# Order of the first loads and of a's first transposes in a two-matmul kernel with GELU between

## The chip, the cores and the metric

The kernel runs on one core of a Trainium2 chip. The metric is the device time of one execution in microseconds, as the median of several executions; smaller is better. A core has a matrix engine (TensorE, PE in the profile, with its weight loads as PEld), three engines for elementwise work (VectorE or DVE, ScalarE or ACT, GpSimd or POOL), and SyncE (SP), which here only issues transfers. Each engine runs its own instructions in order and waits for others at semaphores. Sixteen transfer (DMA) engines move data between the chip's main memory and the on-chip memory SBUF. TensorE writes its results to PSUM, of which there are eight banks of 128 partitions by 512 float32.

## The reference

```python
m, k, n, p = 1024, 1024, 2048, 1024        # a: m x k, b: k x n, c: n x p, float32
h = np.matmul(a, b)
h = 0.5 * h * (1 + np.tanh(np.sqrt(2 / np.pi) * (h + 0.044715 * h ** 3)))
return np.matmul(h, c).astype(np.float32)
```

## The kernel before

The order of all instructions is written out by hand; no scheduler moves them. `a` and `b` are turned into bfloat16. The first product is made transposed, as `hT = gelu(b^T a^T)`, so that TensorE needs `b` as it lies (its weights, 128 by 128) and `a` transposed (`aT`, streamed in 512 columns). `a`'s 1024 rows are two halves of 512 (index h), the contraction of 1024 is eight slices of 128 (index k), and the columns of `b` are tiles of 128 (index t): the first 1024 in `b1`, the others in `b2`. Much later parts, the function `seven` that is used for the rest of the first product and for the second one, multiply blocks of matrices with seven block products in place of eight. They are not touched by the change.

The change is in the start of the kernel, here called phase one: tiles t = 0 to 6 of `b1` against the first half of `a`, over the first half of the contraction, k = 0 to 3. It holds seven PSUM banks open, one for each t, and goes through k from outside, so 7 matmuls of 512 columns follow each slice of `b`, 28 in all (line 128). The eighth bank (7) is for transposes.

Phase one gets its data in float32 over SP's queue. `load_a(k, n)` (L71) brings n slices of 128 columns of `a` for its first 512 rows: 256 KB for one slice in rows of 512 bytes, 512 KB for two in rows of 1024 bytes. `load_b(k, c0, w)` (L74) brings slice k of `b`, `w` of its first 1024 columns: 512 KB, or 256 KB for a half. Eight transfers of 3 MB in all go out without any wait, in the order of lines 76 to 83: a0, the two halves of b0, a1, b1, a2 with a3, b2, b3.

What becomes of them:

- `turn0(k, n)` (L116): DVE casts n slices of `a` to bfloat16 (L118), TensorE transposes them in blocks of 128 by 128 into bank 7 (L122, four for each slice), and DVE copies the bank to `aT` (L124).
- ACT casts the first 512 columns of a slice of `b` (L135; for k = 0 in two pieces of 256), DVE the other 512 (L136).
- TensorE runs seven matmuls (L128) for each k. `turn0(0, 1)` stands ahead of k = 0, `turn0(1, 1)` after the seven of k = 0, `turn0(2, 2)` after the seven of k = 1.

All other loads are issued by POOL and cast to bfloat16 on the way. Ahead of them POOL runs one copy of one element, `gate` (L85), that reads `b`'s slice 1; so POOL's transfers begin when `load_b(1)` has landed. They are, in this order: `a10` and `a11`, the second 512 rows of `a` (L98, two transfers of 256 KB for each half of the contraction), the lower half of `b1` (L105, k = 4 to 7), `a01`, the first 512 rows of `a` for k = 4 to 7 (L98), the other half of `b` (`b2`, L109), and `c` (L112).

After phase one TensorE transposes `a10` (`turn`, L158, copied by DVE at L160), makes tile t = 7 of phase one, and goes on with the second half of `a` (L128 again). ACT and DVE move phase one's seven results to SBUF (`leave`, L147 and L149).

At the very start, ahead of everything, TensorE runs eight matmuls on zeros (L89).

Of the kernel before, what the change touches and what calls it, by code (L numbers as in the profile page):

```python
# [19 lines left out]
def kernel(ctx, tc, a, b, c, out):  # L20
# [22 lines left out]
    def bank(i, shape=(128, H), dt=F32, name="ps"):  # L43
        return pp.tile(list(shape), dt, name=name, tag=f"bank{i}", padded_shape=None)

    def pieces(tag, bufs, shape, dt, name):
        return small.tile(shape, dt, name=name, tag=tag, bufs=bufs)
# [19 lines left out]
    def slice_a(k, n):  # L67
        return sta[:, ds(k * H, n * H)].rearrange("p (mt c) -> p mt c", mt=4)

    def load_a(k, n):  # L70
        nc.sync.dma_start(out=slice_a(k, n), in_=av[:, 0:4, ds(k * 128, n * 128)])  # L71

    def load_b(k, c0=0, w=1024):
        nc.sync.dma_start(out=stb[:, k, ds(c0, w)], in_=bv[:, k, ds(c0, w)])  # L74

    load_a(0, 1)
    load_b(0, 0, H)
    load_b(0, H, H)
    load_a(1, 1)
    load_b(1)  # L80
    load_a(2, 2)
    load_b(2)
    load_b(3)

# [31 lines left out]
    def turn0(k, n):  # L116
        ab = pieces("ab", 2, [128, 4, n * 128], BF16, "ab")
        nc.vector.tensor_copy(ab, slice_a(k, n))  # L118
        pt = bank(7, (128, n, H), BF16, "pt")
        for i in range(n):  # L120
            for j in range(4):
                nc.tensor.transpose(pt[:, i, ts(j, 128)], ab[:, j, ts(i, 128)], ident)  # L122
        for i in range(n):
            nc.vector.tensor_copy(aT[:, 0, k + i], pt[:, i])  # L124

    def mm1(p, t, h, ks, k0=0, k1=KT):
        for k in ks:
            nc.tensor.matmul(p, b1[:, k, ts(t, 128)], aT[:, h, k],  # L128
                             start=(k == k0), stop=(k == k1 - 1))

    turn0(0, 1)
    for k in range(KH):
        for c0 in (0, 256) if k == 0 else (0,):
            w = 256 if k == 0 else H
            nc.scalar.activation(b1[:, k, ds(c0, w)], stb[:, k, ds(c0, w)], AF.Copy)  # L135
        nc.vector.tensor_copy(b1[:, k, H:], stb[:, k, H:])  # L136
        for t in range(N0):
            mm1(ps[t], t, 0, (k,), 0, KH)
        if k < 2:
            turn0(k + 1, k + 1)  # L140


    half = slot("x3", [128, 8, H], F32, "half")
# [268 lines left out]
```

## Time and profile before

| | |
|---|---|
| median of 11 runs | 122.7 us (121.83 to 125.36) |
| the profiled execution, whole | 122.23 us |
| its span in the profile | 120.5 us |
| TensorE matmuls busy | 112.7 us (94%) |
| TensorE weight loads busy | 71.7 us (60%) |
| DVE busy | 88.8 us (74%) |
| ACT busy | 50.8 us (42%) |
| POOL busy | 16.1 us (13%) |
| read from and written to main memory | 20.97 MB, 4.19 MB |

The first table line is the metric; the profile shows one execution, of 122.23 us, of which 120.5 us are the span between its first and its last instruction. Times in the profile are counted from the start of that span. Engines overlap, so busy times don't add up to the span. The profile's lines used below give, for a group of instructions on one engine, the start, the time from the first start to the last end, engine, line of the kernel, operation, what is written from what, the shape, the count, and in brackets how long the engine was idle before and which event ended that.

TensorE's waits before 30 us, as the profile sums them: 1.2 us for the zeros, 1.0 us in two waits for DVE's copies to `aT` (L124), 0.7 us for ACT's cast of `b` (L135), 0.4 us for DVE's cast of `b` (L136), and 0.5 us for the transfer of `a10`. POOL waits 8.7 us at the gate.

### The profile page before, as it was taken

What the parts mean: (1) busy time and instruction counts of PE and PEld (TensorE: products, weight loads), DVE (VectorE), ACT (ScalarE), POOL (GpSimd) and SP (SyncE); (2) the same over time, 40 slices, a digit from 0 to 9 for tenths busy, and PEclk for the clock granted to TensorE, in tenths of its full rate; (3) what the DMA queues carried; (4) which work ended last, traced back from release to release, by engine and by line L of the source; (5) the groups of instructions that cost most, each with busy time, mean ns of one, the idle gap of its engine ahead of it and who ended that gap; (6) DMA issues with size and microseconds to landing.
All of it is one profiled execution on the core that took longest, in us unless ns stands there. A gap on an engine that the chain in (4) does not pass through costs nothing.

```text
span 120.5 us, 1435 instructions
## 1 busy us (share of the span) xinstructions
PE 112.7 (94%) x536; PEld 71.7 (60%) x536; DVE 88.8 (74%) x97; ACT 50.8 (42%) x82; POOL 16.1 (13%) x29
## 2 busy tenths in 40 slices
PE   6787889999999999999999999999999999999970
PEld 2223445644644444888888444468888888888850
DVE  0224577498237899977779999969999996892490
ACT  4102461005537779946669536900012595100000
POOL 2006906853233000000000000000000000000000
PEclk9999999999999999999999999999999999999997
DMA  2899999999999999998000000062000002004695
GB/s 89 187 327 391 185 172 209 206 197 206 207 206 212 212 211 212 210 211 163 5 3 0 0 5 0 0 261 88 0 0 0 0 5 87 0 0 174 237 354 193
DMA packets 11110, 16.34 MB, mean 136 GB/s; under 512 B 736, under 2 KB 5856, under 8 KB 11104
## 3 DMA queue, kind: packets, MB, share of 16 engines
q0 software_dynamic: 6496, 8.91, 42.4%
q1 hardware_dynamic: 4608, 7.34, 17.6%
q8 instruction: 4, 0.07, 0.2%
q14 instruction: 2, 0.02, 0.0%
HBM read 20.97 MB, written 4.19 MB: 209 GB/s over the span
## 4 chain that ended last, share of the span: by engine, by line
PE 71%; DMA 16%; DVE 6%; SPq 1%; issue 1%; POOL 1%; ACT 1%; DVEq 0%; ACTq 0%
PE ps L229 50%; PE ps L128 18%; DMA stb<-in_b_dram 6%; DMA out_dram<-ot 5%; DMA a<-in_a_dram 5%; DVE x L187 4%; PE pt L158 2%; DVE ot L273 2%; SPq L74 1%; SPq L71 1%; POOL a L98 1%; DVE ot L358 1%; ACT u L268 1%; POOL gate L85 0%; DVEq L273 0%
## 5 line engine op out<-in xcount | busy, mean ns | idle before, releaser
L128 PE MATMUL ps<-aT,b 128*128 128x512 bf16 x128 | 30.6, 392 | 2.1 <-DVE aT L124 1.0
L229 PE MATMUL ps<-x,s 128*128 128x512 f32 x128 | 29.6, 391 | 0.0
L229 PEld LDWEIGHTS ps<-x,s 128*128 128x128 f32 x128 | 24.0, 188 | 5.1
L128 PEld LDWEIGHTS <-b 128*128 128x128 bf16 x128 | 12.2, 99 | 17.0 <-ACT b L135 2.5
L229 PE MATMUL ps<-x,x 128*128 128x512 f32 x64 | 14.8, 389 | 0.0
L229 PE MATMUL ps<-c_sb,hT 128*128 128x512 bf16 x64 | 14.0, 379 | 0.0
L229 PEld LDWEIGHTS ps<-x,x 128*128 128x128 f32 x64 | 12.0, 188 | 2.5
L268 ACT ACTIVATE v<-ps 128x512 f32<-128x512 f32 x8 | 4.8, 599 | 17.1 <-PE ps L229 17.1
L163 ACT ACTIVATE hT<-ps 128x512 bf16<-128x512 f32 x12 | 6.8, 594 | 11.3 <-PE ps L128 11.3
L229 PE MATMUL ps<-x 128*128 128x512 f32 x48 | 11.2, 393 | 0.0
L229 PEld LDWEIGHTS <-hT 128*128 128x128 bf16 x64 | 6.2, 98 | 7.6 <-issue 0.3
L229 PEld LDWEIGHTS ps<-x 128*128 128x128 f32 x48 | 9.0, 188 | 1.9
L187 DVE TENSOR_TENSOR x<-c_sb 128x1024 fp32r<-128x1024 bf16 x8 | 9.2, 1216 | 0.0
L273 DVE TENSOR_TENSOR ot<-ps,v 128x512 f32<-128x512 f32 x8 | 5.3, 686 | 4.6 <-DMA out_dram<-ot 3.8
L258 DVE TENSOR_TENSOR half<-ps,half 128x512 f32<-128x512 f32 x8 | 5.5, 691 | 3.2 <-PE ps L128 2.9
L160 DVE COPY aT<-pt 128x1024 bf16<-128x1024 bf16 x6 | 4.1, 689 | 5.1 <-PE pt L158 5.1
L273 DVE TENSOR_TENSOR ot<-ps,u 128x512 f32<-128x512 f32 x8 | 5.4, 689 | 3.0 <-ACT u L268 3.0
L163 ACT ACTIVATE hT<-ot 128x512 bf16<-128x512 f32 x12 | 6.9, 624 | 1.1 <-DVE ot L273 1.1
L229 PE MATMUL ps<-aT,b 128*128 128x512 bf16 x32 | 7.1, 379 | 0.0
L112 POOL DMA_DIRECT2D c_sb<-in_c_dram x8 | 5.7, 711 | 9.7 <-DMA b<-in_b_dram 8.7
L135 ACT ACTIVATE b<-stb 128x512 bf16<-128x512 f32 (+1 forms) x5 | 2.6, 541 | 9.7 <-DMA stb<-in_b_dram 9.7
L268 ACT ACTIVATE p<-ps 128x512 f32<-128x512 f32 x8 | 4.6, 594 | 4.8 <-PE ps L229 4.8
(45 smaller groups left out, 114.6 us busy)
## 6 DMA issues: line engine op xcount, KB each, us to landing
c_sb<-in_c_dram POOLq DMA_DIRECT2D x8, 512.0 KB, 19.6
out_dram<-ot SPq DMA_DIRECT2D x16, 256.0 KB, 2.1
b<-in_b_dram POOLq DMA_DIRECT2D x4, 512.0 KB, 12.4
stb<-in_b_dram SPq DMA_DIRECT2D x3, 512.0 KB, 8.9
a<-in_a_dram POOLq DMA_DIRECT2D x6, 256.0 KB, 7.2
b<-in_b_dram POOLq DMA_DIRECT2D x4, 256.0 KB, 9.3
sta<-in_a_dram SPq DMA_DIRECT2D x2, 256.0 KB, 4.6
stb<-in_b_dram SPq DMA_DIRECT2D x2, 256.0 KB, 5.1
```

Of the source, the lines that this page charges most:

```text
L71: nc.sync.dma_start(out=slice_a(k, n), in_=av[:, 0:4, ds(k * 128, n * 128)])
L112: nc.gpsimd.dma_start(out=c_sb[:, t:t + 2], in_=cv[:, t:t + 2])
L128: nc.tensor.matmul(p, b1[:, k, ts(t, 128)], aT[:, h, k], start=(k == k0), stop=(k == k1 - 1))
L135: nc.scalar.activation(b1[:, k, ds(c0, w)], stb[:, k, ds(c0, w)], AF.Copy)
L158: nc.tensor.transpose(pt[:, n, ts(j, 128)], sts[j // 2][:, j % 2, ts((k + n) % KH, 128)], ident)
L160: nc.vector.tensor_copy(aT[:, h, k:k + 2], pt)
L163: nc.scalar.activation(hT[h][:, t], p, AF.Gelu_apprx_tanh)
L187: nc.vector.tensor_tensor(out=dst[:, r], in0=x[:, r], in1=y[:, r], op=op)
L229: nc.tensor.matmul(p[:, ds(c0, w)], l[:, k, ts(j, 128)], r[:, k, ds(c0, w)], start=(start and k == 0), stop=(k == self.kt - 1), skip_group ...
L258: nc.vector.tensor_tensor(out=half[:, t], in0=p, in1=half[:, t], op=ADD)
L268: nc.scalar.activation(st, p, AF.Copy)
L273: nc.vector.tensor_tensor(out=ot, in0=p, in1=st, op=ADD)
```

## The change

The loads of `a` all go ahead of those of `b` on SP's queue, so the order becomes a0, a1, a2 with a3, the two halves of b0, b1, b2, b3. `turn0(1, 1)` moves from behind the matmuls of k = 0 to ahead of them, and `turn0(2, 2)` from behind those of k = 1 to behind those of k = 0. The gate still reads `b`'s slice 1, and nothing is added or left out. In the changed kernel the lines behind `turn0(1, 1)` have numbers higher by one.

```diff
     load_a(0, 1)
+    load_a(1, 1)
+    load_a(2, 2)
     load_b(0, 0, H)
     load_b(0, H, H)
-    load_a(1, 1)
     load_b(1)
-    load_a(2, 2)
     load_b(2)
     load_b(3)
...
     turn0(0, 1)
+    turn0(1, 1)
     for k in range(KH):
...
         for t in range(N0):
             mm1(ps[t], t, 0, (k,), 0, KH)
-        if k < 2:
-            turn0(k + 1, k + 1)
+        if k == 0:
+            turn0(2, 2)
```

## The prediction

> **What bounds the kernel now.** I read the page's forty slices first, then the chain by engine, TensorE's waits, the chain in order of time, and last the timelines of the first 20 us.
>
> ```profile
> PE   6787889999999999999999999999999999999970
> DMA  2899999999999999998000000062000002004695
> PE 71%; DMA 16%; DVE 6%; SPq 1%; issue 1%; POOL 1%; ACT 1%; DVEq 0%; ACTq 0%
> ```
>
> From the seventh slice to the last two TensorE is full (windows 17.2 to 30 and 30 to 60 us: 12.79 of 12.80 and 30.00 of 30.00 us busy), so what happens before 17.2 us reaches the end one for one, and nothing after it can absorb a delay. What ends last before 17.2 us:
>
> ```profile
> 2.72 7.25 DMA stb<-in_b_dram
> ...
> 10.02 0.18 POOL gate L85
> 10.20 0.76 POOL a L98
> 10.97 6.19 DMA a<-in_a_dram
> ...
> 17.21 0.51 PE pt L158 x6
> ```
>
> The chain is: `load_b(1)` lands (9.97), POOL's one-element copy L85, which waits for that slice, lets POOL's own queue begin (10.02), its first two transfers (a10, L98) are complete at 17.16, and TensorE resumes at 17.21. The matmuls ahead of it are not the bound, but close:
>
> ```profile
> 6.04 1.87 PE L128 MATMUL ps<-aT,b 128*128 128x512 bf16 x4 [0.51 <-DVE aT L124]
> 8.30 1.44 PE L128 MATMUL ps<-aT,b 128*128 128x512 bf16 x3 [0.40 <-DVE b L136]
> 9.55 0.41 PE L122 MATMUL pt<-ident,ab 128*128 128x128 bf16 x4
> 10.68 1.68 PE L128 MATMUL ps<-aT,b 128*128 128x512 bf16 x7 [0.71 <-ACT b L135]
> 12.26 0.62 PE L122 MATMUL pt<-ident,ab 128*128 128x128 bf16 x8
> 13.40 3.18 PE L128 MATMUL ps<-aT,b 128*128 128x512 bf16 x14 [0.52 <-DVE aT L124]
> 16.42 0.28 PE L158 MATMUL pt<-ident,a 128*128 128x128 bf16 x2
> 17.21 0.51 PE L158 MATMUL pt<-ident,a 128*128 128x128 bf16 x6 [0.52 <-DMA a<-in_a_dram]
> ```
>
> The 28 matmuls of phase one end near 16.42; TensorE then loses 0.52 us to a10. Two paces show: at 6.04 to 9.55 a matmul takes (1.44 - 0.61)/2 = 0.42 us start to start (0.61 us: one alone, line L89's rows), from 13.40 on (3.18 - 0.38)/13 = 0.215.
>
> **An arrival clock.** DVE and ACT start their casts when a slice lands:
>
> ```profile
> 3.56 0.43 DVE L118 CAST ab<-sta 128x512 bf16<-128x512 f32 x1 [2.43 <-DMA sta<-in_a_dram]
> ...
> 7.82 0.43 DVE L136 CAST b<-stb 128x512 bf16<-128x512 f32 x1 [1.84 <-DMA stb<-in_b_dram]
> 8.65 0.43 DVE L118 CAST ab<-sta 128x512 bf16<-128x512 f32 x1 [0.40 <-DMA sta<-in_a_dram]
> ...
> 11.50 0.71 DVE L118 CAST ab<-sta 128x1024 bf16<-128x1024 f32 x1 [0.73 <-DMA sta<-in_a_dram]
> ```
>
> With ACT's starts (L135 at 5.50, 9.99, 12.69, 13.94) this gives SP's stream by bytes: 256 KB at 3.56, 512 at 5.50, 768 at 7.82, 1024 at 8.65, 1536 at 9.99, 2048 at 11.50, 2560 at 12.69, 3072 at 13.94. The stream is slow between 3.6 and 7.8 (512 KB in 4.26 us) and then moves 512 KB in 1.3 us. In 3 to 5 us it moves only 140 GB/s, in 8 to 13 us 352.
>
> **The change part by part.** *SP's queue.* The same eight transfers of 3 MB, in another order: a's slices 1 and 2 to 3 (256 and 512 KB) pass both halves of b's slice 0; the second pair also passes b's slice 1. An issue takes 0.43 to 0.50 us here, landings come at least 2.8 us after the issue, so issuing in another order costs nothing: the transfers queue anyway. I take the arrival clock by bytes: a1 5.5, a2-3 8.65, b's first half (8.65 + 9.99)/2 = 9.3, second half 10.0, b1 11.5, b2 12.7, b3 13.9 (the last two as before).
>
> *The gate.* POOL waits for b1; behind that wait stand all of POOL's transfers: a10, a11, b's lower half, a01, b2's quarters, c. It opens at 11.5 instead of 10.0: +1.5 us. Bounds: if the slow stretch vanished, each 256 KB behind a0 (a1, b's two halves) would cost the 0.83 us of 7.82 to 8.65 and each 512 KB (a2-3, b1) the 1.34 of 8.65 to 9.99: 3.56 + 3 x 0.83 + 2 x 1.34 = 8.7, so -1.3 us. If a's short rows met it as well as b's, the 0.5 MB could cost another 0.4 us: 11.9. I take 11.5, since b's own half slices stood in the stretch and still have to come.
>
> *a10 behind the gate.* Before, 17.16 - 10.02 = 7.14 us. Its 2 x 256 KB ran while SP's last slices were landing (to 13.94): 168 GB/s in 13.4 to 17.2 us, against 204 in 17.2 to 30 us alone. 0.524 MB at 168 is 3.12 us, at 204 2.57: up to 0.55 less, because the gate opens later while SP's stream ends when it did. 11.53 + 7.14 - 0.55 = 18.1 (18.7 without that credit). The Trainium skill, "DMA: Bandwidth & Descriptors", Queues, rings and completion order, says each DMA engine takes turns between its queues packet by packet; full turns would halve POOL's rate while both run, and with the last 1.5 us of SP's stream shared the credit would be 0.75 us by an estimate from that rule, which makes it 17.9. The rows here give the two rates only, 168 and 204 GB/s, and the sum uses those.
>
> *TensorE.* `turn0(1, 1)` moves ahead of the first matmuls: one DVE cast (0.43), four transposes (0.41), one copy (0.42), now at about 5.5 to 7.2, in the wait for b's first half, 9.3. They cost nothing there; with b's half at 7 they would delay the matmuls by up to 0.3 (transposes share bank 7 with `turn0(0)` and wait for its copy, 5.56 + 0.42). First matmul: 9.3 + 0.54 (5.50 to 6.04, the cast) = 9.85. Second half: 10.0 + 0.48 (7.82 to 8.30), in time. Seven at 0.42: 12.8. `turn0(2, 2)`: its DVE cast stands behind L137, which waits for the second half (10.0 + 0.43), ready at 11.15, hidden by the seven; eight transposes 0.45 (their weight loads' row). Then 21 matmuls at 0.215 = 4.5, casts of b1 to b3 all ready before: 17.75. Before, fast pace began at 9.55, 3.5 us after the first matmul at 6.04; 3.5 after 9.85 is 13.35, which leaves the eight transposes at half pace, about +0.3: 18.05. So the waits of phase one (0.40, 0.71, 0.52 and the gap before `turn0`) are gone, and the start is 3.8 us later.
>
> The Trainium skill, "TensorE: Matmul & The Clock Gate", Part 1, speaks against the change here: full clock is granted after a busy window of about 3.4 us that runs freely, so the slow stretch may last 3.4 to 6.8 us from the first matmul. By an estimate from that rule the 18.05 could be up to 19.7, in runs where the window falls badly. The row shows one execution only (3.5 us).
>
> *Sum.* TensorE is ready at 18.05, a10 at 18.1, against 17.16 before: resume at 18.15 instead of 17.21, +0.95 us. Downstream nothing becomes late: b's k = 7 (issued 14.7, landing at most 10.7 later, 25.4) is needed at 24.07 + 15 x 0.215 = 27.3, and both shift. The profiled execution took 122.23 (span 120.5, 1.7 around it): 123.2. The median of the runs is 0.47 above it: 123.65. I predict the middle, 123.4.
>
> **The rivals.** (1) *Order costs nothing:* half of what the slow stretch loses, 4.26 - 2 x 0.83 = 2.6 us, is not lost in the new order. b1 lands at 11.5 - 1.3 = 10.2 and a10 at 10.2 + 7.1 = 17.3; b's half at 8.0, first matmul 8.55, seven to 11.5, transposes to 12.25, 21 to 16.75. a10 decides: +0.1 us, 122.3 (122.8 on the median). For it: in 3.5 to 4.5 us the transfer engines are idle for stretches, with transfers queued. Against: 0.5 MB more stand ahead of the gate. (2) *Faster:* the slow stretch belongs to alternating between a and b, and is gone. Gate 8.7, a10 at 8.7 + 7.1 = 15.9; b's half at 3.56 + 0.83 + 1.34 + 0.83 = 6.55, first matmul 7.1, seven to 10.05, transposes to 10.8, 21 more to 15.3. a10 decides: 15.9 against 17.2, -1.3 us, 120.9 (121.4 on the median). For it: 140 GB/s in 3 to 5 us is not what the stream can do. It decides once b1 lands before 9.4. Against: the low rate begins as b's first half moves, not as a's second. (3) *Slow pace longer:* fast pace begins only 6 us or more after 9.85; k = 1's seven cost 7 x 0.205 = 1.4 more and the transposes 0.3: phase one ends at 18.05 + 1.7 = 19.8, +2.6 against 17.2: 124.8 (125.3 on the median). For it: the eight matmuls on zeros from 1.19 and all others until 9.55 were slow. Before, 0.5 us of slack plus data waits hid this. (4) *The change does not reorder what it says:* the instructions as built show all of a ahead of b on SP and both turns ahead on TensorE; no chance kept.
>
> **How the numbers follow.** Forecast 0.43, rival 1 0.20, rival 2 0.17, rival 3 0.20. The forecast's own range is 122.8 (gate 11.0) to 124.2 (no credit, late clock by 0.5). For 8 in 10 I reach into rivals 2 and 3 from both sides: 121.8 to 125.0, which leaves out the far half of each. A measurement tells 0.5%, 0.6 us, from no change: faster 0.17 (rival 2), same 0.20 (rival 1), slower 0.63.
>
> **What would show it.** POOL's gate L85 starting at 11.5; ACT's first cast of b (L136 there) at 9.3; TensorE's seven L128 matmuls in one run from 9.85 without waits; the second half's first transposes (L159 there) going on at 18.1 after a wait on in_a of 0.3 us or less; TensorE full after. Wrong if the gate opens before 10.3, or if phase one ends over 0.5 us after a10 has landed (then the clock decides).

## The result and the profile after

The changed kernel takes 123.95 us (median of 12 runs, 122.89 to 124.39) against 122.24 us for the kernel before (47 runs in all): ratio 1.0131, 95% interval 1.0104 to 1.0158. It is slower, by 1.3%, clear of the noise. Ratios, here and below, leave out the slow executions, those over 1.5% above the fastest of their kernel, so they can differ from the quotient of the medians (here 1.0140). The profiled execution took 123.52 us with a span of 121.8 us, 1.3 us more than before.

The first view is the page's forty slices and the chain's shares by engine, of the changed kernel:

```profile
PE   6718999999999999999999999999999999999970
DMA  3898699999999999999100000053000002004695
PE 76%; DMA 11%; DVE 7%; SPq 1%; issue 1%; ACT 1%; DVEq 0%; ACTq 0%
```

TensorE is emptier in the third slice (6 to 9 us: 1, before 8) and full from the fifth on. DMA's share of the chain fell from 16% to 11%, TensorE's rose from 71% to 76%: the chain left the transfers earlier and stayed on TensorE, but for one stretch on DVE. The chain in order of time (start, length, what) shows where:

```profile
2.30 6.66 DMA stb<-in_b_dram
...
8.99 0.42 ACT b L136
...
9.46 3.17 PE ps L128 x7
12.63 0.87 PE pt L122 x8
...
13.52 0.76 DVE aT L124 x2
14.28 0.34 DVE b L137
...
14.67 3.84 PE ps L128 x17
18.51 0.45 PE pt L159 x8
```

Before, the chain ran from `b`'s slice 1 over POOL's gate to a10. Here it runs from the first half of `b`'s slice 0, landing at 8.97, to TensorE, and stays there but for 1.1 us at 13.5, where it runs over DVE's two copies to `aT` and its cast of `b`'s slice 1. TensorE's waits, summed by the profile:

```profile
PE ps L128 <- ACT b L136: 2.5, 1, 2.5
...
PE ps L128 <- DVE b L137: 0.3, 1, 0.3
```

Four waits in phase one, one of them ahead of its first matmul, became one long wait ahead of it (2.5 us) and one of 0.3 us; the wait for a10 is gone. That does not mean that a10 was early: POOL and its gate (timeline of POOL) show

```profile
11.69 0.18 POOL L85 COPY gate<-stb 128x1 f32<-128x1 f32 x1 [10.39 <-DMA stb<-in_b_dram]
11.81 2.99 POOL L98 DMA_DIRECT2D a<-in_a_dram  x4
```

The gate opens at 11.69 instead of 10.02, and a10's second transfer landed at 18.40 in the trace's landings, before at 17.16. TensorE's matmuls of phase one end their run at 18.35. Both ends came in within 0.05 us of each other, 1.2 us later than a10 before, and tile t = 7 starts at 18.79 instead of 17.55: +1.24 us, which is the span's +1.3 (TensorE's timelines, before and then of the changed kernel):

```profile
17.55 1.03 PE L128 MATMUL ps<-aT,b 128*128 128x512 bf16 x4
```

```profile
18.35 0.61 PE L159 MATMUL pt<-ident,a 128*128 128x128 bf16 x8
18.79 1.03 PE L128 MATMUL ps<-aT,b 128*128 128x512 bf16 x4
```

From there on TensorE is full in both.

### The profile page after: what moved, and what is told of

It reads as the page before. It is cut to its first block, busy times and chain, and to the rows that moved or that the text cites. A ratio compares the mean times of both kernels' runs of the same rounds, so it can differ in the third digit from the quotient of the medians.

```text
span 121.8 us, 1435 instructions
## 1 busy us (share of the span) xinstructions
PE 113.0 (93%) x536; PEld 72.3 (59%) x536; DVE 88.5 (73%) x97; ACT 50.8 (42%) x82; POOL 16.2 (13%) x29
## 4 chain that ended last, share of the span: by engine, by line
PE 76%; DMA 11%; DVE 7%; SPq 1%; issue 1%; ACT 1%; DVEq 0%; ACTq 0%
PE ps L230 50%; PE ps L128 23%; DMA stb<-in_b_dram 5%; DMA out_dram<-ot 5%; DVE x L188 4%; PE pt L159 2%; DVE ot L274 2%; SPq L71 1%; PE pt L122 1%; DVE aT L124 1%; DVE ot L359 1%; ACT u L269 0%; ACT b L136 0%; DVE b L137 0%; DVEq L274 0%
## 5 line engine op out<-in xcount | busy, mean ns | idle before, releaser
L161 DVE COPY aT<-pt 128x1024 bf16<-128x1024 bf16 x6 | 4.0, 687 | 4.5 <-PE pt L159 4.5
```

Of the source, the lines that this page charges most:

```text
L161: nc.vector.tensor_copy(aT[:, h, k:k + 2], pt)
```

## Experiments

Which of the two ends is the loss? All ratios are against the kernel before on the same chip (one for e1 to e4, one for e5 to e7, one for e8 to e11, one for e12).

| label | what | ratio | 95% interval |
|---|---|---|---|
| (the change) | loads and turns | 1.0131 | 1.0104 to 1.0158 |
| e1_loads_only | loads new, turns old | 1.0157 | 1.0104 to 1.021 |
| e2_turns_only | loads old, turns new | 1.0036 | 1.0003 to 1.0068 |
| e3_a1_ahead | only a1 ahead | 1.0206 | 1.015 to 1.0261 |
| e12_a1_timed | the same, timed again | 1.0124 | 1.0054 to 1.0195 |
| e4_warm | change + zeros | 1.0081 | 1.0047 to 1.0115 |
| e5_gate | change + early gate | 1.0155 | 1.0109 to 1.0201 |
| e6_warm_gate | change + zeros + early gate | 1.0047 | 1.0005 to 1.0089 |
| e8_tile7_first | change + tile 7 ahead | 1.0230 | 1.0175 to 1.0285 |
| e9_warm_tile7 | change + zeros + tile 7 ahead | 1.0056 | 1.002 to 1.0091 |
| e7_before_gate | before + early gate | 0.9928 | 0.9888 to 0.9968 |
| e10_gate_tile7 | before + early gate + tile 7 ahead | 0.9983 | 0.995 to 1.0016 |

**The two parts apart.** e1 is the kernel before with the new order of loads alone:

```diff
     load_a(0, 1)
+    load_a(1, 1)
+    load_a(2, 2)
     load_b(0, 0, H)
     load_b(0, H, H)
-    load_a(1, 1)
     load_b(1)
-    load_a(2, 2)
```

> The loads in the new order, the turns of a where they were before. Theory 'two ends' (a10 behind the late gate, 18.40 us in the profile after, and TensorE's late and slow start, 18.35 us, come in together): gate at 11.7, a10 at 18.4, but a1's turn and its copy now stand between the matmuls of k = 0 and k = 1 again, so phase one ends near 18.9: ratio to before 1.013 to 1.019. Rival 'gate alone': a10 at 18.4 decides, 1.010 to 1.013. Rival 'turns alone' (the moved turns cost it, not the loads): 1.000 to 1.004.

Measured 1.0157. Two lines of its timelines, POOL's and TensorE's:

```profile
12.11 0.18 POOL L85 COPY gate<-stb 128x1 f32<-128x1 f32 x1 [10.81 <-DMA stb<-in_b_dram]
```

```profile
19.27 0.61 PE L158 MATMUL pt<-ident,a 128*128 128x128 bf16 x8
```

The gate opened at 12.11, a10 landed at 18.86, and phase one's matmuls gave way to a10's transposes at 19.27 with no wait for a10 (a line with a wait would name it in brackets). So TensorE was the later end, as expected, and the loads alone are enough to make the whole loss.

e2 is the changed kernel with the old order of loads (the diff of e1 the other way round).

> The loads in the old order, the turns of a in the new places. The gate stays at 10.0 and a10 at 17.2 us. Theory 'two ends': TensorE's queue now holds the matmuls of k = 0 behind a1's turn, a1 lands at 8.65, so k = 0 starts near 9.6 at 0.42 us each, and phase one ends at 18.2 to 18.5 although the gate is early: 1.009 to 1.013. Rival 'gate alone': 1.000 to 1.004.

Measured 1.0036, below what the theory expected and inside the rival's range. The expected mechanism is in its profile: first matmul at 9.26, a10's transposes only at 17.99 though a10 was in at 17.11, span 121.4, 0.9 us above the profile of before. But the median moved by 0.41 us only (123.06 against 122.65). The profiled execution of before, 122.23, lies 0.4 us below the median that stood beside e2; why the timed executions differ less than the profiles is not settled.

**The gate held where it was.** In e3 and e12 (one kernel) only a1 goes ahead. The bytes ahead of `b`'s slice 1 are those of before, so the gate should not move, but the first matmuls still come later. The diff is against the changed kernel.

```diff
     load_a(0, 1)
     load_a(1, 1)
-    load_a(2, 2)
     load_b(0, 0, H)
     load_b(0, H, H)
     load_b(1)
+    load_a(2, 2)
...
-        if k == 0:
+        if k == 1:
             turn0(2, 2)
```

> Only a1 goes ahead of b0's halves and a1's turn ahead of the matmuls; a2 with a3 stay behind b1, and their turn behind the matmuls of k = 1. As many bytes ahead of b1 as before, so the gate stays at 10.0 and a10 at 17.2; b0's first half lands near 7.8, k = 0 runs from 8.3 to 11.3, phase one ends at 16.4 to 16.9, ahead of a10: 1.000 to 1.003. Rival 'every late start of the matmuls is paid' (TensorE alone): 2 us later start, 1.006 to 1.012.

Measured 1.0206, a miss, above the rival's range too: in its profile even slice 1 was late, the gate at 11.62. That profile is of the slowest of six executions, 126.25 us. One more profiled execution of the kernel (e11) and then a second timing (e12) followed.

> The kernel with only a1 ahead, once more, for a second profile. If what stands ahead in bytes decides, b1 lands near 10.0 as at first expected and the 11.6 of the first profile was chance; if the order makes it, b1 lands at 11.0 or later again.

One execution, 122.57 us, gate at 10.26: the late gate of the first profile was not the order's. Its phase one ended at 17.27, and a10 was in at 17.44.

> The kernel with only a1 ahead of b's slices, timed again, since its six executions at first lay at 1.021 with b1 landing at 11.6, and a single one later at 122.57 us with b1 landing at 10.2, TensorE going on at 17.3 without a wait for a10. If the order of a1 and b0 does cost 1.5 to 2% by itself, 1.012 to 1.026 again; if the first series was a slow stream of its own, 1.000 to 1.008.

Measured 1.0124, in the range for a cost that the order of a1 and b0 makes by itself, and above the 1.000 to 1.003 that e3 was expected to give. The profile of e12, timelines of POOL and of TensorE:

```profile
10.17 0.44 POOL L85 COPY gate<-stb 128x1 f32<-128x1 f32 x1 [8.86 <-DMA stb<-in_b_dram]
```

```profile
8.65 5.72 PE L128 MATMUL ps<-aT,b 128*128 128x512 bf16 x14 [1.67 <-ACT b L136]
14.20 0.61 PE L122 MATMUL pt<-ident,ab 128*128 128x128 bf16 x8
15.33 3.18 PE L128 MATMUL ps<-aT,b 128*128 128x512 bf16 x14 [0.52 <-DVE aT L124]
18.35 0.61 PE L159 MATMUL pt<-ident,a 128*128 128x128 bf16 x8
```

The gate is where it was before, within 0.15 us, a10 landed at 17.19, as before, and yet a10's transposes start at 18.35, the very time of the changed kernel. The cause stands in the first line: 14 matmuls in 5.72 us. The last 14 take 3.18. At the full pace of 0.215 us and the slow one of 0.427, (5.72 - 3.18) / 0.212 = 12 of the 13 steps were slow: the full pace came only 12 x 0.427 = 5.1 us after the first matmul. In e11, with the same instructions, 14 took 4.97 us: the first two steps were at the full pace, then the granted clock was half from 8.94 to 12.35. In e12 the late start is paid for as long as the slow pace lasts, and the gate has no part in it.

**The slow pace taken away.** e4 is the changed kernel with more matmuls on zeros:

```diff
-    for _ in range(8):
+    for _ in range(12):
         nc.tensor.matmul(wps, warm[:, 0:128], warm, start=True, stop=True)
...
     turn0(1, 1)
+    for _ in range(10):
+        nc.tensor.matmul(ps[6], warm[:, 0:128], warm, start=True, stop=True)
     for k in range(KH):
```

> The changed kernel with 12 matmuls on zeros at the start instead of 8 and 10 more behind a1's turn, so that TensorE's pace is full when b's first half is cast. Theory 'two ends': phase one is done by 16.3 to 17, TensorE then waits over 1 us for a10 at 18.4, and the time stays: 1.010 to 1.014. Rival 'TensorE alone' (the slow pace makes the loss): 1.000 to 1.005.

Measured 1.0081: between the two ranges. TensorE's timeline in e4:

```profile
10.47 1.67 PE L128 MATMUL ps<-aT,b 128*128 128x512 bf16 x7
...
17.45 0.27 PE L161 MATMUL pt<-ident,a 128*128 128x128 bf16 x2
18.95 0.51 PE L161 MATMUL pt<-ident,a 128*128 128x128 bf16 x6 [1.23 <-DMA a<-in_a_dram]
```

The seven matmuls of k = 0 now take 1.67 us, not 3.17, TensorE is done at 17.45, and then it does wait 1.23 us for a10 at the late gate's mercy. So a10 is a second end close behind the first, and 0.8% stays. This execution, 124.02 us, was the slowest of ten (median 123.36), so its wait for a10 (landed at 18.91) was probably longer than in most; and the ten added matmuls ran until 10.47, some 0.4 us past the first cast of `b`.

**a10 brought earlier.** e5 and e6 open the gate at the second half of `b`'s slice 0, e5 in the changed kernel, e6 in e4:

```diff
-    nc.gpsimd.tensor_copy(gate, stb[:, 1, 0:1])
+    nc.gpsimd.tensor_copy(gate, stb[:, 0, H:H + 1])
```

> The changed kernel with POOL's gate on the second half of b's slice 0 (landing at 10.3) in place of slice 1 (11.7). a10 lands near 17.1 to 17.5 us, but TensorE still ends phase one at 18.3 or later, since b's last slices share the transfer engines with POOL's: theory 'two ends': 1.011 to 1.017. Rival 'gate alone': a10 1 us earlier is 1 us gained, 1.002 to 1.006.

> The changed kernel with both: the extra matmuls on zeros and the gate on the second half of b's slice 0. Theory 'two ends': only with both moved does the time fall, phase one done by 17, a10 by 17.1 to 17.5: 0.999 to 1.005. Under 'gate alone' it is like the kernel with the early gate alone, under 'TensorE alone' like the one with the zeros alone.

Measured 1.0155 and 1.0047, both in their ranges. But e5 does not test what it was made for: the gate opened 1.3 us earlier, but a10 came later, not earlier. Two lines of its timelines, POOL's and TensorE's:

```profile
10.41 0.44 POOL L85 COPY gate<-stb 128x1 f32<-128x1 f32 x1 [9.11 <-DMA stb<-in_b_dram]
```

```profile
19.22 0.51 PE L159 MATMUL pt<-ident,a 128*128 128x128 bf16 x6 [0.62 <-DMA a<-in_a_dram]
```

From gate to a10 it took 8.8 us here, 6.7 in the changed kernel. In the trace's landings 15 of 16 transfer engines had finished their part of a10 by 17.86 and one at 19.17; the last one counts. In e6's profile it was the same: gate at 10.37, a10 at 19.01, a wait of 1.78 us for it. e6 lies below e4 by 0.34%, inside their intervals, and its twelve executions spread widely, from 121.99 to 124.41; the quotient of the plain medians, 123.52 and 122.34, is 1.0096.

e8 and e9 cover the wait for a10 instead: tile t = 7, which needs none of it, goes ahead of a10's transposes, in e8 in the changed kernel, in e9 in e4.

```diff
-    turn(a10, 1, 0, 0)
     p7 = bank(7)
     mm1(p7, 7, 0, range(KH), 0, KH)
     leave(7, p7)
+    turn(a10, 1, 0, 0)
```

> The changed kernel with tile t = 7 of phase one (four matmuls, 0.86 us, that need nothing of a10) ahead of a10's first transposes, so that a wait for a10 up to 0.86 us is covered, at the price of a bare copy after the transposes, some 0.4 us. Theory 'two ends', with a10 and TensorE within 0.2 us of each other in most executions: no gain, 1.011 to 1.017. If a10 comes in 0.5 us or more behind TensorE in most executions (rival 'gate alone'): 1.006 to 1.011.

> Extra matmuls on zeros (TensorE at full pace, phase one done at 17.4) and tile t = 7 ahead of a10's transposes (a wait of up to 0.86 us covered). Theory 'two ends': both covered, 1.001 to 1.007, below either alone (1.008 for the zeros). Rival 'TensorE alone': as with the zeros alone, or 0.4 us above it for the bare copy, 1.007 to 1.012.

Measured 1.0230 and 1.0056. e8 is above its range. In its profile nothing was there to cover: a10 was in at 17.91, and the 28 matmuls ended near 18.2. The bare copy behind the transposes (a wait of 0.3 us for L161) was added, but that makes 0.3% where e8 lies 1.0% above the changed kernel. The rest is not explained; the slow pace in e8's profile lasted until 14.6, 5.6 us after the first matmul. e9 meets its range and lies 0.25% below e4, inside the intervals.

Taken in pairs, the zeros gain each time: 1.0131 to 1.0081, 1.0155 to 1.0047, 1.0230 to 1.0056, in the last two pairs with intervals clear of each other (by the plain medians 1.0140 to 1.0058, 1.0162 to 1.0096, 1.0194 to 1.0043). The granted clock of the timed executions, averaged over the span, fits that. In the profiles it is 0.986 or less only where TensorE got the full pace and lost it again (e2, e11, e8; lines in the last section). In six of the changed kernel's twelve executions and in all seven of e8 it is 0.965 to 0.986, in all 34 of e4, e6 and e9 0.993 or more. The measures for a10 gain nothing without the zeros, and with them nothing clear of the intervals.

**The kernel before with an early gate.** e7 takes the gate from `b`'s slice 1 to a1 in the kernel before, e10 adds tile 7 ahead.

```diff
-    nc.gpsimd.tensor_copy(gate, stb[:, 1, 0:1])
+    nc.gpsimd.tensor_copy(gate, sta[:, H:H + 1])
```

> The kernel before with POOL's gate on a's slice 1 (landing at 8.65) in place of b's slice 1 (10.0). TensorE waited 0.5 us for a10 there. If a10 is what bounds the kernel before, it lands near 16.2 to 16.6 and phase one ends at 16.5 to 16.9 with b's last slices a little late: 0.994 to 0.999. If sharing costs b's slices what a10 gains: 1.000 to 1.004.

> The kernel before with the gate on a's slice 1 and tile t = 7 ahead of a10's transposes. Phase one ends at 16.3, tile 7 at 17.2; if a10 lands near 17.2 as in the profile of the early gate alone, 0.3 us better than that kernel: 0.988 to 0.993. If a10 is mostly in by 16.5 there, the bare copy costs 0.4 us: 0.994 to 0.999.

e7 measured 0.9928 (0.9888 to 0.9968): one line makes it faster than both kernels. Its profile does not show the gain: a10 landed at 17.16 there, as before, and that execution, 122.28 us, was the second slowest of ten (median 121.36). That of e10 does show an early a10: in at 15.63, ahead of the end of phase one's 28 matmuls (15.8), span 119.7. So there the tile ahead had nothing to cover, and its bare copy cost a wait of 0.34 us: 0.9983, above e7 on another chip, with intervals that just overlap.

## Why the prediction was right, point by point

**The bound before.** Right that the stretch up to 17.2 us reaches the end one for one: tile 7 +1.24 us, span +1.3.

**The arrival clock.** It held where it mattered. `b`'s first half was predicted for 9.3, its cast started at 8.99; second half 10.0 and 10.30; slice 1 11.5 and 11.66; slice 2 12.7 and 12.93; slice 3 13.9 and 14.19. Between these points it did not hold: a2 with a3 were expected at 8.65 and landed at 7.32, and `b`'s first half then took 1.65 us more for its 256 KB. That the two errors nearly cancelled at 8.97 is luck. The reason given for choosing it was wrong: the slow stretch is not `b`'s. These are the rates over 3 to 9 us, 40 slices of 0.15 us, of the kernel before, of e1 and of the changed kernel:

```profile
GB/s 260 328 314 205 27 27 14 55 41 55 68 164 259 232 300 324 273 277 307 249 311 242 324 369 287 260 317 297 273 369 331 253 328 348 406 382 348 328 403 355
```

```profile
GB/s 345 348 345 355 280 24 14 20 82 48 157 280 300 335 389 396 375 396 389 396 348 266 232 259 164 137 96 109 232 287 246 232 232 287 218 205 273 232 259 300
```

```profile
GB/s 212 311 290 300 263 120 150 140 123 229 229 280 294 307 300 225 246 355 348 341 321 328 314 273 307 314 273 287 259 164 246 314 150 177 355 219 355 328 369 314
```

All three dip between 3.6 and 4.7 us, before with `b`'s rows in flight, the others with `a`'s, less deeply in the changed kernel. The stream pays it whatever stands second, and e1 and the changed kernel have a second, shallower one where `b` begins. (The prediction's 0.43 to 0.50 us for an issue holds for six of the eight before; the last two took 1.12 and 0.56 us, which cost nothing, since their transfers queued.)

**The gate and a10.** Gate 11.5 predicted, 11.69 measured; a10 18.1 and 18.40. The credit of 0.55 us for less sharing came to 0.43 here: 6.71 us from gate to landing against 7.14 before; the 17.9 by the rule of turns was further off. But the delay has no fixed size: with the same order of loads and the same gate it was 6.75 us in e1, 6.95 in e8, 6.76 in e9 and 7.25 in e4, and with the earlier gate of e5 8.8.

**TensorE.** First matmul 9.85 predicted, 9.46 measured; the seven 2.95 and 2.96 us; the turn of a2 and a3 0.75 and 0.86, all eight transposes at the slow pace, which lasted 4.0 us from the first matmul (3.5 taken from the kernel before, 3.4 to 6.8 allowed for); end of the run 18.05 and 18.35. One step of the sum failed, "casts of b1 to b3 all ready before". DVE's timeline in the changed kernel:

```profile
13.52 0.76 DVE L124 COPY aT<-pt 128x512 bf16<-128x512 bf16 x2 [2.19 <-PE pt L122]
14.19 1.18 DVE L137 CAST b<-stb 128x512 bf16<-128x512 f32 x3
```

Slice 1 had landed at 11.63, but its cast on DVE stands in the queue behind the two copies of a2's and a3's turn, which wait for the transposes. Four matmuls of k = 1 ran at 13.28 and the other three had to wait until 14.67. The fourth started at 13.28 + 1.11 - 0.38 = 14.01 (0.38 us is the length of one), so 14.23 was possible for the fifth: 0.44 us lost. Moving `turn0(2, 2)` ahead of k = 1 put a wait ahead of that cast, and the prediction looked at what stands behind L137 at k = 0 only.

**The sum.** +0.95 us was predicted, the profiles differ by 1.3 and the medians by 1.7. The mechanism was right and the size too small: in the profile both ends came 0.3 us later than in the sum. On TensorE's side the cast behind the copies (0.44), the slower turn (0.11) and 0.14 among the last 21 matmuls stand against a first matmul 0.39 earlier; on a10's side it is the gate (0.2) and the delay behind it (0.1). Either side alone would have held TensorE to about 18.4, so the cast by itself is not what made the loss larger. The other 0.4 us, between profiles and medians, is not explained: the profiled execution of the changed kernel was the third fastest of twelve, that of the kernel before stood at the median. The forecast of 123.4 lies within 0.5% of 123.95 partly by luck: it starts from the 122.7 of 11 runs, and the 47 runs put the kernel before at 122.24.

**The rivals.** The third, a longer slow pace, is no separate case: in e12 it lasted 5.1 us and there the late start with it cost, without the gate, about what the whole change costs. The forecast put both ends level and named the gate first; the runs put TensorE's late, slow start first. Rival 2 needed the slow stretch to vanish, rival 1 needed 1.3 us of it to be saved. Neither came: 1.3 us were in hand when a2 with a3 landed at 7.32, but they were lost again where `b` began, and slice 1 landed at 11.63, not at rival 1's 10.2. That the order as built is the one described was right.

What remains open: how much of the 1.3% is a10 alone, since opening the gate earlier did not bring a10 earlier in the changed kernel, why e2 lost less than its profile, and why e8 lost more than its copy.

## What to carry to other kernels

Loading one operand wholly ahead delays the first matmul by all its bytes (here from 6.04 to 9.46 us); even where the sum of transfers stays, the matmul engine then starts late, in most traces here slow as well (4.0 us in the changed kernel's), and it has no slack left to meet the next transfer. When a step moves ahead, read what it puts in front of each later instruction on every engine's queue, not only on the matmul engine's. Where a small wait is the bound (a10 here), try the trigger of that transfer first: one line gave 0.7% in e7. Then read when the transfer lands: in the changed kernel the same step, in e5, brought it no earlier.

## What the runs showed of the hardware that was not expected

The full pace of TensorE comes at very different times. Before, it came 3.5 us after the first matmul on data, in e12 5.1 us. In e10, with the same eight matmuls on zeros as before, it was there from the first matmul on data on (TensorE's timeline of e10; four steps of 0.22 us and not 0.42):

```profile
6.00 1.04 PE L128 MATMUL ps<-aT,b 128*128 128x512 bf16 x4 [1.02 <-ACT b L135]
```

The trace's record of the granted clock has the full pace from 9.59 us on before, from 13.79 in e12 and from 3.98, still in the zeros, in e10. Up to its first entry that record reads as full (1.00 in the view of windows), although the steps are of 0.42 us.

The full pace is also taken back. In e8 it was there from 4.33 us, through the transposes, and went at 7.75, in the wait for `b`. Windows of e8 (from and to, length, TensorE's busy time and count, granted clock, share of the transfer engines, GB/s):

```profile
4.40:7.70 3.30, 1.01 (x9) 1.00 1.02 329
7.80:14.50 6.70, 5.53 (x20) 0.50 0.79 247
14.60:18.00 3.40, 3.40 (x18) 1.00 1.08 167
```

In e2 (from 5.91) and e11 (from 5.53) the full clock lasted 3.41 us and the half clock behind it 3.41 us as well; in e8 the half clock lasted 6.83. TensorE had been busy for 0.3 to 1.0 us of the stretch that ended with the loss; in e10, 1.9 us in the 3.41 us from 3.98 on went without a loss. No idle time in e11 ahead of the loss was longer than 1.55 us.

The Trainium skill, "TensorE: Matmul & The Clock Gate", Part 1, says that the activity window runs freely, so that where a kernel's start falls in it changes from run to run; the 0, 3.5 and 5.1 us here agree with that.

The transfer of a10 is as late as its slowest transfer engine: in e5 one of 16 came 1.3 us after the others. An earlier start of a queue that shares the engines with another did not make it land earlier in e5 (gate 10.41, landing 19.17) nor in the profiles of e6 (10.37, 19.01) and e7 (8.45, 17.16); in e10 (7.72, 15.63) it did.
